# A hybrid decoder block on one core: another order of the seven products in closing Strassen steps, and the convolution's product four steps later

## The chip, the cores and the metric

The kernel runs on 1 core of one Trainium2 chip. The metric is the device time of one execution in microseconds (us), the median over the runs; lower is better.

## The reference

One decoder block on x of 256 tokens by 4096 channels in float32. Six kinds of projection come out of one matrix `w_in`; a pooling branch and a convolution branch are built from them, each goes through its own 2048x4096 matrix, sigmoid gates merge the two, and `w_out` and a norm close the block.

```python
h = rmsnorm(x, norm_w)
proj = h @ w_in                                   # 256 x 4096 by 4096 x 20480
u_p, z_p, u_c, b_c, c_c, z_c, g_logit = split(proj)
y_pool = (pooled(u_p) @ pool_w per group) * pool_scale * silu(z_p)   # trailing windows 2, 4, 8, 16
v = c_c * u_c
y_conv = b_c * (conv_b + sum(conv_w[k] * v shifted by 2-k, k = 0..2)) * silu(z_c)
br = [y_pool @ w_branch[0], y_conv @ w_branch[1]]  # each 256 x 2048 by 2048 x 4096
merged = sum(sigmoid(g_logit + gate_b) * br)
x = x + merged @ w_out                            # 256 x 4096 by 4096 x 4096
return rmsnorm(x, final_norm_w)
```

## The kernel before

**Units.** All the matrix work is cut into 31 units of 1024 output columns, one behind another. In order: `cz0 cb0 cu0 cc0 cz1 cb1 cu1 cc1` (the convolution branch: z, b, u and c projections of its two halves), `pz0 pu0 pz1 pu1` (the pooling branch), `g0_0 g0_1 g1_1 g0_2 g1_2 g0_3 g1_3 g1_0` (gates), `b0_0 b1_0 ... b0_3 b1_3` (branch matrices) and `o0 o1 o2 o3` (`w_out`). A unit is a row of 16 steps (8 in the `b` units). A step takes 256 rows of the weights: a 2x2 grid of 128x512 blocks, multiplied by a 2x2 grid of 128x128 blocks of the activations (two token halves by two row halves).

**Steps.** Every float32 operand is split into a rounded high part (type fp32r) and the rest, the low part, and a product is three matmuls: high by high, high by low, low by high. A P step does the eight block products plainly: 24 matmuls, into four PSUM banks, the E banks (t, n) for token half t and column half n, named `sums_82` (0,0), `sums_83` (0,1), `sums_84` (1,0) and `sums_85` (1,1). An S step does one round of Strassen's scheme in seven products: 21 matmuls, into three E banks (all but (1,0)) and four further banks, the F banks `shared_86` to `shared_89`. Three of the seven, N6, N4 and N7, need sums of weight blocks that VectorE (DVE) forms first (tile `parts`). Strings such as `"PPPPSPSPSSPSSPSS"` (L38 to L51) give each unit's steps; an S step that ends a unit is a *closing* step.

**Preparing a step.** SyncE loads the weights (`raw`: 768 KB, and a corner of 256 KB; for an S step GpSimd adds a second block into the corner by an accumulating DMA). ScalarE (ACT) writes the high parts into cells of `ring` (26 cells of 128x512), DVE the low parts, and in an S step DVE forms `parts`, ACT their highs (`ring<-parts`), DVE their lows. A step's cells are handed out in the order of the program, up to four steps ahead, where cells are free (`pump`, L1049).

**Closing a unit.** After each product, `after_group` (L1102) looks which banks are complete. A complete E bank is copied out by ACT at once (`evacuate`, L425: `E<-sums` or `Y<-sums`), a complete F bank by ACT into tile `J` (`copy_corners`, L431: `J<-shared`). These copies stand in ACT's queue in the order in which the banks close, among the high parts of the following steps. Every unit begins with a P step, which writes E bank (0,1) with its first three matmuls, (1,1) with the next three, then (0,0) and (1,0); a bank can be written again when its copy is done.

**Epilogues.** What a unit still has to do on ACT, DVE and the DMA queues is put into a queue of small items, one per *tick* of 6 matmuls (`tick`, L1084), so that it runs beside the next unit. Of `cc0` and `cc1` these are transposes, the taps of the convolution (`taps`, L590) and in the end `whole` (L605), the product of convolution and gate, `E<-J,Y`, four times 128x512. `gate_unit` (L718) puts two DMAs that add the bias rows (`E<-in_rows_dram`, GpSimd's queue) and 12 ticks later two sigmoids on ACT. `side_items` (L553) makes two extra Strassen operands of x after `cz0`.

**Operands.** The activations' operands for the `b` and `o` units come back from DRAM (`fills`, `Fill.advance`, L820): a transfer into a stage (`sa`, `sb`, `sc`), for an S operand four sums on DVE into a scratch tile `four` (one, the lower half of `sa`), highs on ACT (`arena<-`), lows on DVE.

**Start and end.** 18 matmuls of zeros (`WARM`, L33, L922) keep TensorE (PE) busy before the first weights arrive. At the end, `finish_half` (L1244) adds a half of the last columns and squares it, `finish` (L1251) forms the inverse root of the mean square and scales four tiles, which go out by DMA; it is done for token half 0, then for 1.

Of the kernel before, what the change touches and what calls it, by code (L numbers as in the profile page):

```python
# [54 lines left out]
def hybrid_block(ctx: ExitStack, tc: tile.TileContext, x, xc, prm, rows_in, w_in, pool_w, w_branch, w_out, out):  # L55
# [208 lines left out]
    class Step:  # L264
# [85 lines left out]
        def groups(self):  # L350
            gs = []
            if self is steps[0]:
                for k in (1, 0):
                    for n in (1, 0):
                        h, l, free = self.plain(2 * (1 - k) + 1 - n)
                        for i in range(3):
                            for t in range(2):
                                ah, al = self.op.standing(k, t)
                                gs.append([("E", t, n), [((ah, h), (al, h), (ah, l))[i]], ()])
                        gs[-1][2] = free  # L360
            elif self.kind == "P":
# [140 lines left out]
    def gap(n):  # L502
        return [None] * n
# [24 lines left out]
    def seq_x(text):  # L528
        if text is FIRST:
            return [("P", i) for i in FIRST]  # L530
        text = [c for c in text if c in "PS"]
        ns = text.count("S")
        if ns > NS + NB:
            ss = list(range(ND, 16)) + [resident[0]]
            if ns > NS + NB + 1:
                resident[0] = 2 * ND - 3 - resident[0]
                ss = [ss[-1]] + ss[:-1] + [resident[0]]
            ps = [i for i in range(ND) if i not in ss]
            return [(c, (ss if c == "S" else ps).pop(0)) for c in text]
        return sequence(text, ND, ND + NS + NB, NB)  # L540
# [9 lines left out]
    def side_load(i):  # L550
        aside(side["tile"], side_d[i - ND + 2])

    def side_items(i):  # L553
        def scaled():
            for k in range(2):
                v = sa[:, 6 - 2 * k:8 - 2 * k]
                act(v, v, scale=norm_col(2 * i + k))

        return [lambda: move(sa[:, 4:].rearrange("p o c -> p (o c)"), xc[i])] + gap(7) + [scaled, None, lambda: sums_s(sa)] + gap(3) + [
            lambda: act(side["tile"][:, 0], sa[:, 0:4]), None,  # L560
            lambda: sub(side["tile"][:, 1], sa[:, 0:4], side["tile"][:, 0].bitcast(F32)),
            None, None, None, None, lambda: aside(side_d[i - ND + 2], side["tile"])]

    def silu_y(late):
        def silu(t):
# [7 lines left out]
    def conv_units(c, first):  # L573
        base = 2 * HALF + c * NU

        def b_epi(u):
            def product(t):
                stt(E[:, t], E[:, t], rin[:, t:t + 1], Y[:, t], ALU.mult, ALU.mult)
            return gap(15) + [lambda: product(0), None, lambda: product(1)] + gap(5) + [lambda: move(g_d[c], E)]

        def c_epi(u):
            def inner(j):
                if j == 3:
                    for i in range(4):
# [28 lines left out]
        u = in_unit(f"cz{c}", base + 3 * HALF, lambda u: silu_y(u.late) + (gap(4) + side_items(ND - 1) + side_items(ND - 2) if first else []),  # L613
                    FIRST if first else EIGHT4, dst=Y)
        u.late = not first
        in_unit(f"cb{c}", base + HALF, b_epi, TEN if c else NINE_A).late = True
# [157 lines left out]
    def out_unit(c):  # L774
# [15 lines left out]
        text = (SEVEN4, NINE, NINE, OUT3)[c]  # L790
# [19 lines left out]
    class Fill:  # L810
        def __init__(self, o, src, free, ready):
            self.o, self.free, self.ready, self.src = o, free, ready, src
            self.at = self.st = None
            self.phase = self.due = 0

        def fetch(self, st):
            self.at, self.st = now[0], st
# [2 lines left out]
        def advance(self, force):  # L820
            o, q = self.o, self.st
            n = o.n - 4 if o.kind == "S" else 0
            four = sa[:, 0:4]
            if self.phase == 0 and n and any(f.phase and f.o.kind == "S" for f in fills):
                return False
            if not force and (now[0] < self.due or (self.phase != 1 and now[0] < quiet[0])):
                return False
            if self.phase == 0 and o.kind == "S":
# [20 lines left out]
                rested[id(self.st)] = now[0] + REST  # L849
            return True  # L850

    stages = [sa[:, 4:8]]
    fills = deque()
    now, quiet, hush = [0], [0], [0]
    LANDING, STORED, QUIET, HUSH, REST = 8, 7, 5, 20, 5
# [312 lines left out]
    for u in units:  # L1168
        if u.name == "b0_0":
            last_pair["stack"].close()  # L1170
            open_last(F32)
        if u is names["o1"]:
            assert not fills
            more.close()
            open_side()

# [11 lines left out]
        if u is last_x:  # L1188
            side["stack"].close()
            more = ExitStack()  # L1190
            ctx.enter_context(more)
            pool = more.enter_context(tc.tile_pool(name="more", bufs=1))
            apart["tile"] = pool.tile([P, 8 * P], F32R, name="apart")
            stages.extend(pool.tile([P, 4, P], F32, name=name) for name in ("sb", "sc"))
            queue_fills()
        if u is last:
            break
# [46 lines left out]
    def finish_half(t, n):  # L1244
# [3 lines left out]
            accum_out=ossq[:, t, 3 + n:4 + n])  # L1248
        mul(rest[:, t, cs], E[:, t, cs], Y[:, 0, cs])

    def finish(t):  # L1251
# [11 lines left out]
    for t in range(2):  # L1263
        for ns in ((0, 1),) if t == 0 else ((0,), (1,)):
# [49 lines left out]
```

## Time and profile before

| | |
|---|---|
| median of 3 runs | 2348.76 us (2348.66 to 2349.11) |
| the profiled execution's own time | 2348.53 us |
| its span, first to last instruction | 2346.8 us |
| granted TensorE clock | 0.999 |
| instructions in the trace | 29867 |

A row of the timeline says: start in us from the span's start, length in us, engine (PE is TensorE's matmuls, PEld its weight loads), line, operation, out<-in, shape, how many of them were merged into the row, and in brackets how long the engine idled before it and what ended that. A matmul row's length runs to the modelled end of its last matmul (389 ns for one of 512 columns), while the next begins earlier: the pace is read from starts, or from a row of many. Line 1096 is the helper `multiply`, lines 62 and 65 the helpers of ACT and of DVE, so the names of the tiles tell what a row is.

### The profile page before, as it was taken

The numbers are of one execution on the slowest core, as the hardware profiler recorded it, in microseconds if no ns is written. First come the engines' busy times: TensorE is split into PE (matmuls) and PEld (weight loads), VectorE is DVE, ScalarE is ACT, GpSimd is POOL, SyncE is SP. The second block draws the span as 40 slices with busy tenths as digits, with TensorE's granted clock in tenths as the row PEclk, the third lists the DMA queues.
The fourth block names the chain that finished last, engine by engine and source line by source line (L and its number), as shares of the span: only waits on it lengthen the run. The fifth ranks groups of instructions, "written<-read, shape, count | busy, mean of one in ns | idle before, by whom it ended". The sixth has DMA issues, their size and how long they took to land.

```text
span 2346.8 us, 29867 instructions
## 1 busy us (share of the span) xinstructions
PE 2332.0 (99%) x10382; PEld 1930.1 (82%) x10382; DVE 2134.0 (91%) x2177; ACT 1539.8 (66%) x1926; POOL 298.7 (13%) x362
## 2 busy tenths in 40 slices
PE   9999999999999999999999999999999999999998
PEld 7888888888888888888888888888888888878886
DVE  8789999999989979979999899998999889999898
ACT  6666656666666656667766766666676667666664
POOL 0111101111101101101121111111011010011110
PEclk9999999999999999999999999999999999999999
DMA  9789978989978868868999999999889889889998
GB/s 376 247 250 291 273 229 248 282 246 284 271 219 256 264 201 252 257 205 255 290 275 276 307 284 284 278 309 288 277 271 279 273 266 295 272 237 303 290 268 288
DMA packets 203975, 634.60 MB, mean 270 GB/s; under 512 B 21424, under 2 KB 29872, under 8 KB 201008
## 3 DMA queue, kind: packets, MB, share of 16 engines
q1 hardware_dynamic: 134912, 485.42, 59.0%
q0 software_dynamic: 51264, 105.40, 24.7%
q10 hardware_dynamic: 17648, 41.87, 4.9%
q8 instruction: 81, 1.33, 0.2%
q14 instruction: 70, 0.57, 0.1%
HBM read 585.42 MB, written 25.17 MB: 260 GB/s over the span
## 4 chain that ended last, share of the span: by engine, by line
PE 95%; DVE 3%; ACT 1%; issue 1%; DMA 0%; DVEq 0%; SPq 0%; ACTq 0%
PE sums L1096 67%; PE shared L1096 26%; DVE ring L65 2%; PE shared L705 1%; PE shared L483 1%; DVE parts L65 1%; DVE E L65 0%; ACT ring L62 0%; DVE Y L77 0%; DMA raw<-in_w_in_dram 0%; ACT J L62 0%; DVE raw L1259 0%; PE shared L681 0%; ACT Y L62 0%; PE shared L682 0%
## 5 line engine op out<-in xcount | busy, mean ns | idle before, releaser
L1096 PE MATMUL sums<-ring,arena 128*128 128x512 f32 x6732 | 1611.3, 390 | 2.9 <-ACT arena L62 1.3
L1096 PEld LDWEIGHTS sums<-ring,arena 128*128 128x128 f32 x6732 | 1262.2, 188 | 267.2 <-DVE ring L65 2.9
L65 DVE TENSOR_TENSOR ring<-raw,ring 128x512 fp32r<-128x512 f32 (+2 forms) x979 | 1091.8, 1140 | 143.9 <-PE sums L1096 57.5
L62 ACT ACTIVATE ring<-raw 128x512 fp32r<-128x512 f32 (+1 forms) x942 | 899.3, 1015 | 89.6 <-PE sums L1096 65.0
L62 ACT ACTIVATE ring<-parts 128x1024 fp32r<-128x1024 f32 (+1 forms) x493 | 399.7, 823 | 542.8 <-DVE parts L65 487.7
L1096 PE MATMUL shared<-ring,arena 128*128 128x512 f32 x2319 | 590.1, 389 | 0.0
L1096 PEld LDWEIGHTS shared<-ring,arena 128*128 128x128 f32 x2319 | 435.3, 188 | 90.3
L65 DVE TENSOR_TENSOR ring<-parts,ring 128x1536 fp32r<-128x1536 f32 (+2 forms) x274 | 416.7, 1533 | 4.8 <-ACT ring L62 4.6
L92 POOL DMA_DIRECT2D raw<-in_w_in_dram x178 | 153.9, 864 | 1369.2 <-DMA raw<-in_w_in_dram 518.1
L65 DVE TENSOR_TENSOR parts<-raw,parts 128x1024 f32<-128x1024 f32 x236 | 288.5, 1222 | 0.0
L65 DVE TENSOR_TENSOR parts<-raw 128x512 f32<-128x512 f32 x236 | 162.9, 690 | 2.2
L65 DVE TENSOR_TENSOR J<-J 128x512 f32<-128x512 f32 (+1 forms) x90 | 78.3, 870 | 15.1 <-ACT J L62 12.5
L62 ACT ACTIVATE E<-sums 128x512 f32<-128x512 f32 x76 | 42.1, 596 | 47.1 <-PE sums L1096 46.1
L62 ACT ACTIVATE J<-shared 128x512 f32<-128x512 f32 x128 | 68.3, 620 | 6.6 <-PE shared L1096 6.4
L1096 PE MATMUL sums<-ring,last_pair 128*128 128x512 f32 x261 | 66.1, 389 | 0.0
L1096 PE MATMUL shared<-ring,side 128*128 128x512 f32 x261 | 66.0, 389 | 0.0
L1096 PE MATMUL shared<-ring,last_pair 128*128 128x512 f32 x252 | 63.6, 389 | 0.0
L92 POOL DMA_DIRECT2D raw<-in_w_out_dram x33 | 28.7, 870 | 273.8 <-DVE ring L65 142.5
L92 POOL DMA_DIRECT2D raw<-in_w_branch_dram x25 | 21.7, 869 | 287.7 <-DVE ring L65 69.0
L1096 PEld LDWEIGHTS shared<-ring,side 128*128 128x128 f32 x261 | 49.0, 188 | 10.2
L1096 PEld LDWEIGHTS sums<-ring,last_pair 128*128 128x128 f32 x261 | 49.0, 188 | 10.2
L1096 PEld LDWEIGHTS shared<-ring,last_pair 128*128 128x128 f32 x252 | 47.3, 188 | 9.8
(133 smaller groups left out, 729.6 us busy)
## 6 DMA issues: line engine op xcount, KB each, us to landing
raw<-in_w_in_dram SPq DMA_DIRECT2D x318, 768.0 KB, 6.9
raw<-in_w_in_dram SPq DMA_DIRECT2D x326, 256.0 KB, 6.0
raw<-in_w_branch_dram SPq DMA_DIRECT2D x64, 768.0 KB, 7.2
raw<-in_w_out_dram SPq DMA_DIRECT2D x64, 768.0 KB, 7.1
raw<-in_w_in_dram POOLq DMA_DIRECT2D x178, 256.0 KB, 6.7
raw<-in_w_branch_dram SPq DMA_DIRECT2D x64, 256.0 KB, 5.6
raw<-in_w_out_dram SPq DMA_DIRECT2D x64, 256.0 KB, 6.0
E<-J POOLq DMA_DIRECT2D x30, 512.0 KB, 10.3
```

The lines of the kernel that those rows point to most:

```text
L62: return pin(nc.scalar.activation(dst, src, func, **kw))
L65: return pin(nc.vector.tensor_tensor(out=dst, in0=a, in1=b, op=op))
L92: return pin(nc.gpsimd.dma_start(dst, src, accum_op=ALU.add))
L483: pin(nc.tensor.transpose(shared(j)[:, i * T + t * P:i * T + (t + 1) * P], src[:, t, c:c + P], ident))
L705: pin(nc.tensor.matmul(o, a, b, start=(k, i) == (0, 0), stop=(k, i) == (3, 2)))
L1096: pin(nc.tensor.matmul(ps, lhs, rhs, start=n == 0, stop=n == u.total[b] - 1))
```

## The change

Six things are changed; what is computed is the same.

1. Closing S steps multiply in the order M2 N3 M1 N5 N4 N7 N6 (before: M2 N3 N4 M1 N7 N5 N6). The three products of formed sums now come last, so E bank (1,1), which N4 completes, closes fifth and not third.
2. `whole`, the convolution's product, is queued later: gaps of 12, 2, 3, 3 items ahead of its four parts (before 2, 2, 2, 2).
3. `cb0` gets ten S steps (before nine), `o0` six (before seven). `cb0` therefore uses both extra operands of x, and `side_items` makes both with one chain of items.
4. During `b1_3` and `o0` the fills have three scratch tiles for sums (before one), two of them in the place of the tile `apart`, which is closed earlier.
5. `WARM` is 23 (before 18).
6. `finish` does part of the mean square ahead (`partial`, three small DVE instructions after the first half), folds the rest into the square root's bias and drops one multiplication.

```diff
-WARM = 18
+WARM = 23
...
-NINE_A = "PSPSSPSPSSPSPSPS"
+TEN_B = ("PSPSSPSSP", "SSPSSPS")
...
-SEVEN4 = "PPPPSPSPSPSPSSPS"
+SIX5 = "PPPPPSPSPSPSPSPS"
...
-                order = ("M2", "N3", "N4", "M1", "N7", "N5", "N6") if self.closing else (
+                order = ("M2", "N3", "M1", "N5", "N4", "N7", "N6") if self.closing else (
                     "N5", "M2", "N3", "M1", "N6", "N7", "N4")
...
+        if text is TEN_B:
+            ss = list(range(ND, 13)) + [ND - 1] + list(range(13, 16)) + [ND - 2]
+            ps = list(range(ND - 2))
+            return [(c, (ss if c == "S" else ps).pop(0)) for c in "".join(text)]
...
-            for j in range(4):
-                items += gap(2) + [lambda j=j: whole(j)]
-            return items + gap(5) + [lambda: put(y_d[1, c], chan(E))]
+            for j, n in enumerate((12, 2, 3, 3)):
+                items += gap(n) + [lambda j=j: whole(j)]
+            return items + gap(4) + [lambda: put(y_d[1, c], chan(E))]
...
-            four = sa[:, 0:4]
-            if self.phase == 0 and n and any(f.phase and f.o.kind == "S" for f in fills):
-                return False
+            if self.phase == 0 and n:
+                used = [f.four for f in fills if f.phase and f.o.kind == "S"]
+                self.four = next((q for q in fours if not any(q is u for u in used)), None)
+                if self.four is None:
+                    return False
+            four = self.four
...
+        if u is names["b1_3"]:
+            lone.close()
...
+            fours.extend(pool.tile([P, 4, P], F32, name=name) for name in ("sd", "se"))
...
+    def partial(t):
+        b, h = known[:, t, 0:1], known[:, t, 1:2]
+        pin(nc.vector.tensor_reduce(out=b, in_=ossq[:, t, 0:4], axis=mybir.AxisListType.X, op=ALU.add))
+        pin(nc.vector.tensor_scalar(out=b, in0=b, scalar1=1.0 / D, scalar2=EPS, op0=ALU.mult, op1=ALU.add))
+        pin(nc.vector.tensor_scalar(out=h, in0=b, scalar1=-0.5, scalar2=None, op0=ALU.mult))
+
     def finish(t):
         r = rout[:, t:t + 1]
-        rstd_of(ossq[:, t:t + 1], r, f"rout{t}")
+        b, h, q, s = (known[:, t, i:i + 1] for i in range(4))
+        act(s, ossq[:, t, 4:5], AF.Sqrt, scale=1.0 / D, bias=b)
+        stt(h, ossq[:, t, 4:5], -0.5 / D, h, ALU.mult, ALU.add)
+        pin(nc.vector.reciprocal(out=r, in_=s))
+        stt(q, r, h, r, ALU.mult, ALU.mult)
+        stt(r, q, 1.5, r, ALU.add, ALU.mult)
...
             for n in ns:
                 finish_half(t, n)
+            if 0 in ns:
+                partial(t)
         finish(t)
```

The change moves instructions. First, ScalarE's queue at the border from unit `g1_3` to `g1_0`, before: `E<-sums` are the copies of E banks, `J<-shared` of F banks, `ring<-raw` the high parts of a later step.

```order
L62 ACTIVATE E<-sums_83 128x512
L62 ACTIVATE E<-sums_82 128x512
L62 ACTIVATE E<-sums_85 128x512
L62 ACTIVATE J<-shared_86 128x512
L62 ACTIVATE J<-shared_88 128x512
L62 ACTIVATE J<-shared_87 128x512
L62 ACTIVATE ring<-raw 128x1536
L62 ACTIVATE ring<-raw 128x512
L62 ACTIVATE J<-shared_89 128x512
```

The same place in the changed kernel:

```order
L62 ACTIVATE E<-sums_83 128x512
L62 ACTIVATE E<-sums_82 128x512
L62 ACTIVATE J<-shared_86 128x512
L62 ACTIVATE J<-shared_87 128x512
L62 ACTIVATE ring<-raw 128x1536
L62 ACTIVATE ring<-raw 128x512
L62 ACTIVATE E<-sums_85 128x512
L62 ACTIVATE J<-shared_88 128x512
L62 ACTIVATE J<-shared_89 128x512
```

The copy of bank `sums_85` has moved from the third place to the seventh, behind two copies of F banks and, here, behind the two instructions that make the high parts of a later step. At the border from `g1_0` to `b0_0` it stands behind the same four; from `b0_3` to `b1_3` behind two copies and an `arena<-sb`; at the other borders behind a closing S step behind the two copies alone.

Second, VectorE's queue in the middle of `cz1`, before; `E<-J,Y` is `whole`, `ring<-raw` and `ring<-parts` are low parts.

```order
L65 TENSOR_TENSOR E<-J,Y 128x512
L65 TENSOR_TENSOR parts<-raw 128x512
L65 TENSOR_TENSOR ring<-raw,ring 128x512
L65 TENSOR_TENSOR parts<-raw,parts 128x1024
L65 TENSOR_TENSOR E<-J,Y 128x512
L65 TENSOR_TENSOR ring<-raw,ring 128x1536
L65 TENSOR_TENSOR ring<-parts,ring 128x1536
L65 TENSOR_TENSOR ring<-raw,ring 128x1536
L65 TENSOR_TENSOR ring<-raw,ring 128x512
L65 TENSOR_TENSOR E<-J,Y 128x512
L65 TENSOR_TENSOR parts<-raw 128x512
```

The same steps in the changed kernel:

```order
L65 TENSOR_TENSOR parts<-raw 128x512
L65 TENSOR_TENSOR ring<-raw,ring 128x512
L65 TENSOR_TENSOR parts<-raw,parts 128x1024
L65 TENSOR_TENSOR ring<-raw,ring 128x1536
L65 TENSOR_TENSOR ring<-parts,ring 128x1536
L65 TENSOR_TENSOR ring<-raw,ring 128x1536
L65 TENSOR_TENSOR ring<-raw,ring 128x512
L65 TENSOR_TENSOR parts<-raw 128x512
L65 TENSOR_TENSOR ring<-raw,ring 128x512
L65 TENSOR_TENSOR parts<-raw,parts 128x1024
L65 TENSOR_TENSOR E<-J,Y 128x512
```

The second S step of the pair (its `parts`, then `ring<-raw` of 1536 and `ring<-parts`) and the P step behind it have no `whole` among them any more; the first `whole` stands in the S step that follows.

More of the change, by code (lines that the diff above doesn't have):

```diff
@@ L551, in side_load, with side_items, fetch, made @@
         aside(side["tile"], side_d[i - ND + 2])
[L553 to L562, printed above, removed]
+    def side_items(a, b):
+        def fetch(i):
+            return lambda: move(sa[:, 4:].rearrange("p o c -> p (o c)"), xc[i])
+        def made(i):
+            def scaled():
+                for k in range(2):
+                    v = sa[:, 6 - 2 * k:8 - 2 * k]
+                    act(v, v, scale=norm_col(2 * i + k))
+            def high():
+                st = next(s for s in steps[16:] if s.op is x_ops[a] and s.kind == "S")
+                assert i == a or state["now"] > steps.index(st)
+                act(side["tile"][:, 0], sa[:, 0:4])
+            return [scaled, None, lambda: sums_s(sa)] + gap(3) + [
+                high, None, lambda: sub(side["tile"][:, 1], sa[:, 0:4], side["tile"][:, 0].bitcast(F32))]
+        def keep(i):
+            return lambda: aside(side_d[i - ND + 2], side["tile"])
+        return [fetch(a)] + gap(7) + made(a) + [fetch(b)] + gap(3) + [keep(a)] + gap(3) + made(b) + gap(4) + [keep(b)]
     def silu_y(late):
@@ L607, in whole @@
                 mul(chan(E)[:, b], chan(J)[:, b], chan(Y)[:, b])
-            for j in range(4):
-                items += gap(2) + [lambda j=j: whole(j)]
-            return items + gap(5) + [lambda: put(y_d[1, c], chan(E))]
-        u = in_unit(f"cz{c}", base + 3 * HALF, lambda u: silu_y(u.late) + (gap(4) + side_items(ND - 1) + side_items(ND - 2) if first else []),
+            for j, n in enumerate((12, 2, 3, 3)):
+                items += gap(n) + [lambda j=j: whole(j)]
+            return items + gap(4) + [lambda: put(y_d[1, c], chan(E))]
+        u = in_unit(f"cz{c}", base + 3 * HALF, lambda u: silu_y(u.late) + (gap(4) + side_items(ND - 1, ND - 2) if first else []),
                     FIRST if first else EIGHT4, dst=Y)
         u.late = not first
-        in_unit(f"cb{c}", base + HALF, b_epi, TEN if c else NINE_A).late = True
+        in_unit(f"cb{c}", base + HALF, b_epi, TEN if c else TEN_B).late = True
         u = in_unit(f"cu{c}", base, lambda u: rescale(Y), TEN, dst=Y)
@@ L788, in epi @@
                 lambda: mul(E, E, Y[:, 0:1].to_broadcast([P, 2, NU]))] + gap(4) + [lambda: move(o_d[c], E)]
-        text = (SEVEN4, NINE, NINE, OUT3)[c]
+        text = (SIX5, NINE, NINE, OUT3)[c]
         u = Unit(f"o{c}", lambda i: w_out[c, i], seq_x(text), m_ops, epi, before=start if c == 3 else None)
@@ L814, in __init__ @@
             self.phase = self.due = 0
+            self.four = None
         def fetch(self, st):
@@ L850, in advance @@
             return True
-    stages = [sa[:, 4:8]]
+    stages, fours = [sa[:, 4:8]], [sa[:, 0:4]]
     fills = deque()
@@ L1171, in hybrid_block @@
             open_last(F32)
+        if u is names["b1_3"]:
+            lone.close()
+            lone = ExitStack()
+            ctx.enter_context(lone)
+            pool = lone.enter_context(tc.tile_pool(name="lone", bufs=1))
+            fours.extend(pool.tile([P, 4, P], F32, name=name) for name in ("sd", "se"))
         if u is names["o1"]:
             assert not fills
+            lone.close()
             more.close()
@@ L1192, in hybrid_block @@
             pool = more.enter_context(tc.tile_pool(name="more", bufs=1))
-            apart["tile"] = pool.tile([P, 8 * P], F32R, name="apart")
             stages.extend(pool.tile([P, 4, P], F32, name=name) for name in ("sb", "sc"))
+            lone = ExitStack()
+            ctx.enter_context(lone)
+            apart["tile"] = lone.enter_context(tc.tile_pool(name="lone", bufs=1)).tile([P, 8 * P], F32R, name="apart")
             queue_fills()
```

1 line of the change is left out of this document (added).

## The prediction

> **What bounds the kernel now.** I read the page's busy times first, then PE's own waits, then the timeline at each place where PE loses time.
>
> ```profile
> span 2346.8 us, 29867 instructions
> PE 2332.0 (99%) x10382; PEld 1930.1 (82%) x10382; DVE 2134.0 (91%) x2177; ACT 1539.8 (66%) x1926; POOL 298.7 (13%) x362
> ...
> PE sums L1096 <- ACT arena L62: 1.3, 1, 1.3
> ...
> 24.01 9.00 PE L1096 MATMUL sums<-ring,arena 128*128 128x512 f32 x39
> ```
>
> PE is the bound: busy 99%, and the longest of its listed waits is 1.3 us. Its pace is (9.00 - 0.39)/38 = 0.2267 us for a matmul of 512 columns. Only two things can move the time: the number of matmuls, and moments in which PE loses time. DVE is close behind at 91%, so what delays DVE or ACT can become a new moment of that kind. All sums below are made against the profiled execution's own 2348.53 us (span 2346.8); the runs' median 2348.76 lies 0.23 above it, and I add that at the end. A measurement of this kernel can tell about 0.2%, 4.7 us, from no change.
>
> **The number of matmuls.** `cb0` gains an S step and `o0` loses one; each swap is 24 - 21 = 3 matmuls, 0.68 us, once down and once up: 0. DVE's load moves along (an S step has more lows and sums); in `cb0` it is covered by DVE's slack, and the `TEN` units already run ten S steps beside PE without a wait in the list.
>
> **Stalls that the change takes away.** In the timeline, PE and DVE in the middle of `cz1`, PE at the like place of `pz0`, then a step of `pz1` and one of `g0_0`, and the last step of `o0`:
>
> ```profile
> 385.61 0.70 DVE L65 TENSOR_TENSOR E<-J,Y 128x512 f32<-128x512 f32 x1
> 386.21 1.76 DVE L65 TENSOR_TENSOR ring<-raw,ring 128x1536 fp32r<-128x1536 f32 x1
> 387.37 0.39 PE L1096 MATMUL sums<-ring,arena 128*128 128x512 f32 x1
> 388.03 1.42 PE L1096 MATMUL sums<-ring,arena 128*128 128x512 f32 x5 [0.27 <-DVE ring L65]
> ...
> 713.92 0.39 PE L1096 MATMUL sums<-ring,arena 128*128 128x512 f32 x1
> 714.62 1.43 PE L1096 MATMUL sums<-ring,arena 128*128 128x512 f32 x5 [0.31 <-DVE ring L65]
> ...
> 923.51 1.14 PE L1096 MATMUL sums<-ring,arena 128*128 128x512 f32 x3
> ...
> 1102.19 1.19 PE L1096 MATMUL sums<-ring,arena 128*128 128x512 f32 x3
> ...
> 2082.78 3.11 PE L1096 MATMUL sums<-ring,last_pair 128*128 128x512 f32 x13
> 2085.97 0.61 ACT L62 ACTIVATE arena<-sa 128x512 fp32r<-128x512 f32 x1
> 2087.16 2.69 PE L1096 MATMUL sums<-ring,arena 128*128 128x512 f32 x9 [1.27 <-ACT arena L62]
> ```
>
> *cz1, pz0.* The second matmul of a product waits for lows that DVE ends at 386.21 + 1.76 = 387.97, because `whole` stood ahead of them. Loss: 388.03 - 387.37 - 0.23 = 0.43, and 1.42 - (0.39 + 4 x 0.2267) = 0.12 in the row itself: 0.55; in `pz0` 0.47 + 0.13 = 0.60. In the order three of the four `whole` (each 0.60 from start to start) now stand behind these lows, 1.8 us of room where 0.6 is missing. They come later among steps whose lead they shorten, but never beyond what it is today, since by the third S pair all four are done in either kernel. I take the whole gain, -1.15; bounds -1.15 and 0 (the stall comes back a step later).
>
> *pz1, g0_0.* Three matmuls should take 0.39 + 2 x 0.2267 = 0.84 and take 1.14 and 1.19: N4 waits for the lows of formed sums. N4 now comes two products (1.36 us) later: -0.30 - 0.35 = -0.65.
>
> *o0.* The 13 end their issue at 2082.78 + 13 x 0.2267 = 2085.73; the next starts at 2087.16 (1.43 late), and its nine take 2.69 instead of 2.20 (0.49): 1.92. The closing step's operand was filled last, its highs only at 2085.97, behind the one scratch tile. In the changed order its sums no longer wait for another fill to let go of that tile, and one S step less goes before it: for DVE one instruction of 1536 lows (1.76, as at 386.21) and the two that form `parts` less. I take -1.92; bounds -1.92 and -1.2, the second if DVE writes this fill's two lows (0.69 us each today) just too late.
>
> **The start.** PE's first rows, and the third step's weights:
>
> ```profile
> 1.12 4.02 PE L923 MATMUL shared<-warm 128*128 128x256 bf16 x18 [1.12 <-DVE warm L919]
> 6.02 16.11 PE L1096 MATMUL sums<-ring,arena 128*128 128x512 f32 x63 [0.88 <-DVE ring L802]
> ...
> 15.33 2.01 ACT L62 ACTIVATE ring<-raw 128x1536 fp32r<-128x1536 f32 x2 [1.78 <-DMA raw<-in_w_in_dram]
> 16.86 2.36 DVE L65 TENSOR_TENSOR ring<-raw,ring 128x1536 fp32r<-128x1536 f32 x2
> 18.67 1.46 PEld L1096 LDWEIGHTS sums<-ring,arena 128*128 128x128 f32 x7 [0.16 <-DVE ring L65]
> ```
>
> A warm-up matmul takes about 0.21 us, so five more fill the idle 0.88 us to within 0.2. The 63 real ones should take 0.39 + 62 x 0.2267 = 14.44 and take 16.11: 1.67 us lost, most of it in the first microseconds at half pace. The Trainium skill ("TensorE: Matmul & The Clock Gate", section "What's actually happening") says that the array runs at half clock until a free-running window of about 3.4 us was busy; by it a gap-free warm-up would release the clock about when the real work starts, and up to 1.5 us would go out of the sum. The trace agrees as far as it goes: behind the gap of 0.88 the work starts slow. I don't take that gain: the third step needs lows that DVE starts at 16.86 and ends 1.76 later, at 18.6, tied to a load whose landing ended ACT's wait at 15.33, and PE is there at 18.67 already with 0.16 of waiting. A faster first step waits there. -0.1; bounds -1.5 (if those loads also come earlier) and +0.2 (five extra at 0.21 against 0.88).
>
> **What the new order of products costs.** E bank (1,1) closes two products later, its copy goes to the back of ACT's queue, and the next unit's second product, three matmuls in, writes that bank. ACT and PE at three borders (`g1_3` to `g1_0`, `g1_0` to `b0_0`, `b0_3` to `b1_3`) and at that of `pz1`:
>
> ```profile
> 1585.22 1.56 ACT L62 ACTIVATE E<-sums 128x512 f32<-128x512 f32 x3
> 1586.65 1.59 ACT L62 ACTIVATE J<-shared 128x512 f32<-128x512 f32 x3
> 1588.08 2.05 ACT L62 ACTIVATE ring<-raw 128x1536 fp32r<-128x1536 f32 x2
> 1589.97 0.65 ACT L62 ACTIVATE J<-shared 128x512 f32<-128x512 f32 x1
> 1587.39 4.92 PE L1096 MATMUL sums<-ring,arena 128*128 128x512 f32 x21
> ...
> 1667.59 1.26 ACT L62 ACTIVATE E<-sums,rin 128x512 f32<-128x512 f32 x2
> 1668.73 0.70 ACT L62 ACTIVATE E<-sums,rin 128x512 f32<-128x512 f32 x1
> 1669.67 4.70 PE L1096 MATMUL sums<-ring,arena 128*128 128x512 f32 x20
> ...
> 1960.74 2.00 ACT L62 ACTIVATE ring<-raw 128x512 fp32r<-128x512 f32 x2
> 1962.64 0.59 ACT L62 ACTIVATE E<-sums 128x512 f32<-128x512 f32 x1
> 1964.81 3.56 PE L1096 MATMUL sums<-ring,arena 128*128 128x512 f32 x15
> ...
> 925.38 1.55 ACT L62 ACTIVATE Y<-sums 128x512 f32<-128x512 f32 x3
> 927.23 1.98 PE L1096 MATMUL sums<-ring,arena 128*128 128x512 f32 x8
> ```
>
> From start to start a copy takes 0.48 (1585.22 to 1586.65 in three), one scaled by `rin` 0.57, the pair of highs 1.89 (1588.08 to 1589.97). Queued behind the copy and so late with it: the last two `J` copies and the highs of the next step; PE waits for the copy itself.
>
> *g1_3:* copies at 1585.22 and 1585.70, `J` at 1586.17 and 1586.65, highs from 1587.13 to 1589.02, then bank (1,1), done 0.6 later at 1589.6. PE wants it at 1587.39 + 0.68 = 1588.07: +1.55. *g1_0:* copies at 1667.59 and 1668.16, `J` at 1668.73 and 1669.21, highs to 1671.58, copy done at 1672.28, wanted at 1670.35: +1.93. *b0_3:* an `arena` high of 0.5 now ahead of the highs puts the first copy at 1963.16, the second at 1963.64, `J`, `J` and another `arena` follow, the copy starts at 1965.6 and ends at 1966.2, wanted at 1965.49: +0.70. *pz1, g0_0:* copies from 925.38, bank (1,1) fifth, at 925.38 + 4 x 0.48 = 927.3, done at 927.9, wanted at 927.23 - 0.30 + 0.68 = 927.61: +0.3 each, which eats the gain there. *cc0, cc1:* as `g1_0` without the highs, 1.93 - 1.89: +0.1 for both. At the other borders the same count ends before PE asks. Sum +4.9. No row of the trace shows PE waiting for such a copy; bounds 0, if ACT gets to these copies earlier than today, and +6, if each is late by a further 0.1 to 0.2.
>
> **The end.** DVE's second half add, ACT's root and the scaling of the last half:
>
> ```profile
> 2336.05 0.68 DVE L65 TENSOR_TENSOR E<-sums,E 128x512 f32<-128x512 f32 x1
> ...
> 2337.72 0.15 DVE L930 TENSOR_SCALAR rout_m<-rout_m 128x1 f32<-128x1 f32 x1
> 2337.91 0.20 ACT L62 ACTIVATE rout_s<-rout_m 128x1 f32<-128x1 f32 x1 [0.41 <-DVE rout_m L930]
> ...
> 2338.92 1.54 DVE L1259 TENSOR_SCALAR raw<-raw,rout 128x512 f32<-128x512 f32 x3
> ```
>
> Small DVE instructions stand 0.19 apart. Two before the root and one behind it go: -0.6. But for token half 1 the three of `partial` stand in DVE's queue ahead of the add at 2336.05, and PE has that half done by then (DVE is the late one): +0.6. The sum is 0; bounds -0.4 and +0.3.
>
> **The sum.** -1.15 - 0.65 - 1.92 - 0.1 + 4.9 + 0 = +1.1 us: 2349.6 for an execution like the profiled one, 2349.9 for the median.
>
> **The rivals.**
>
> *The copies cost nothing.* For it: ACT idles a third of the time. Against: at these borders it has no idle row, it runs copies and highs back to back. Sum -3.8: 2345.0. Still within 0.2%.
>
> *The same, and a full pace from the first matmul is kept.* If the array, busy without a gap, runs at full pace from 6.02 and the third step's load lands as much earlier, the 1.67 lost go, less the 0.16 of waiting and up to 0.2 of longer warm-up: -1.3 more, 2343.7, faster. The row at 18.67 speaks against it.
>
> *Slower: the bias rows.* GpSimd's queue, the profile's DMA issues and ACT in `g1_3`:
>
> ```profile
> 1549.20 1.19 POOL L92 DMA_DIRECT2D E<-in_rows_dram  x1
> E<-in_rows_dram POOLq DMA_DIRECT2D x14, 512.0 KB, 10.3
> 1559.66 1.99 ACT L62 ACTIVATE E<-E 128x1024 f32<-128x1024 f32 x2
> ```
>
> In six gate units one corner load now stands ahead of both bias transfers, so both start where the second did, and the second lands later. Today it lands at about 1549.2 + 10.3 = 1559.5, and its sigmoid starts at 1560.6. If it lands a whole transfer after the first, at 1569.8, ACT stands some 5 us with the highs behind it. Cover: the order also puts that sigmoid four highs (about 4 us) further back, to 1564.6, and PE's lead over the lows takes up 2 more. It decides from a landing 7 us after the first; then about 3 us in each of six units: 2368.
>
> *The change doesn't do what it says:* the three waits on lows and fills stay or come back next door, the copies cost as above: +1.1 + 3.7 = +4.8: 2353.6, just slower.
>
> **How the numbers follow.** Forecast 0.72, free copies 0.13, free copies and clock 0.05, bias rows 0.04, stalls that stay 0.06. Likeliest: 2349.9. From 2344.9 to 2353.0 the range holds the forecast with its bounds (about 2347.5 to 2352) and the free copies; the last three cases lie outside. Faster by over 0.2% is the clock case, 0.05; slower is the bias rows and most of the last, 0.08; the rest, 0.87, is within 0.2%.
>
> **What would show it.** Right: in the profile after, PE waits for `E<-sums` or ACT at the starts of `g1_0`, `b0_0` and `b1_3`, 1.5, 1.9 and 0.7 us, and the gaps at 387, 714 and 2087 us are gone; the first 63 matmuls end as today, with a wait for DVE in the third step. Wrong: no PE gap at those starts; a third step that starts a microsecond earlier; sigmoids that wait for `E<-in_rows_dram`; or a time beyond the range.

## The result, and the profile after

| | before | after |
|---|---|---|
| median, each of 5 runs side by side | 2348.80 us | 2358.76 us (2357.97 to 2359.44) |
| ratio, with its 95% interval | | 1.004 (1.0028 to 1.0052) |
| the profiled execution's own time | 2348.53 us | 2357.97 us |
| its span | 2346.8 us | 2356.2 us |

The kernel became 0.4% slower. The forecast was 2349.9, within 0.2% of before, with a range up to 2353.0: wrong, by 8.9 us.

From the page of the changed kernel, the busy times and the two groups of matmuls that take their weights from `last_pair` (count, busy time, mean ns of one, idle time ahead):

```profile
span 2356.2 us, 29866 instructions
PE 2338.0 (99%) x10387; PEld 1929.2 (82%) x10387; DVE 2134.1 (91%) x2166; ACT 1541.7 (65%) x1918; POOL 294.9 (13%) x362
...
L1116 PE MATMUL sums<-ring,last_pair 128*128 128x512 f32 x261 | 68.7, 396 | 0.5 <-DVE ring L65 0.3
L1116 PE MATMUL shared<-ring,last_pair 128*128 128x512 f32 x252 | 65.9, 397 | 0.0
```

The same two groups on the page of before:

```profile
L1096 PE MATMUL sums<-ring,last_pair 128*128 128x512 f32 x261 | 66.1, 389 | 0.0
...
L1096 PE MATMUL shared<-ring,last_pair 128*128 128x512 f32 x252 | 63.6, 389 | 0.0
```

PE is busy 6.0 us more with five warm-up matmuls more and no real one: the 513 matmuls of the two groups take longer, 396 to 397 ns in the mean instead of 389. What PE waits for, of the changed kernel:

```profile
PE sums L1116 <- ACT E L62: 3.9, 3, 1.8
PE sums L1116 <- DVE ring L65: 1.6, 2, 1.3
PE shared L943 <- DVE warm L939: 1.1, 1, 1.1
```

The first row is the forecast's late copies; the wait for `arena`, 1.3 us before, is gone. PE and ACT at the starts of `g1_0`, `b0_0` and `b1_3`, where the prediction put them:

```profile
1593.61 0.62 ACT L62 ACTIVATE E<-sums 128x512 f32<-128x512 f32 x1
...
1594.29 3.03 PE L1116 MATMUL sums<-ring,arena 128*128 128x512 f32 x12 [1.47 <-ACT E L62]
...
1678.13 0.71 ACT L62 ACTIVATE E<-sums,rin 128x512 f32<-128x512 f32 x1
...
1678.89 1.45 PE L1116 MATMUL sums<-ring,arena 128*128 128x512 f32 x5 [1.81 <-ACT E L62]
...
1975.06 1.20 PE L1116 MATMUL sums<-ring,arena 128*128 128x512 f32 x4 [0.62 <-ACT E L62]
```

A unit's length, from its first matmul's start to the next unit's, is the finest measure of all: worked out from the starts in the trace, it repeats to 0.02 us from one execution to another where nothing waits (80.24 in every undisturbed unit of 354 matmuls). The differences, after less before:

| term | forecast | measured |
|---|---|---|
| a step on `last_pair` in 24 of the 32 units (80.24 became 80.43) | none | 24 x 0.193 = +4.6 |
| late copy, `g1_0`, `b0_0`, `b1_3` | +1.55 +1.93 +0.70 | +1.79 +2.15 +0.82 |
| late copy, starts of `cz1 pz0 cb1 pu0 pu1 g0_1` | +0.7 (0.1 for `cz1 pz0`, 0.6 for `pu1 g0_1`) | +1.81 (0.53, 0.62, and 0.66 for `cb1 pu0`) |
| waits inside `cz1` and `pz0` | -1.15 | -0.14 |
| N4 in `pz1` and `g0_0` | -0.65 | -0.78 |
| last step of `o0` | -1.92 | -1.85 |
| start and `cz0`, less its step on `last_pair` | -0.1 | +0.70 |
| from the last product to the end | 0 | +0.3 |

These and +0.09 of `b1_1` come to +9.5, and so do the spans (2356.25 less 2346.77). The list of units ahead of the prediction has 32 names, not 31. In a unit with no wait at all, `cu1`, the 21 matmuls of the step on `last_pair`, before:

```profile
566.78 0.84 PE L1096 MATMUL sums<-ring,arena 128*128 128x512 f32 x3
567.46 0.84 PE L1096 MATMUL shared<-ring,last_pair 128*128 128x512 f32 x3
568.14 1.52 PE L1096 MATMUL sums<-ring,last_pair 128*128 128x512 f32 x6
569.50 2.20 PE L1096 MATMUL shared<-ring,last_pair 128*128 128x512 f32 x9
571.54 0.84 PE L1096 MATMUL sums<-ring,last_pair 128*128 128x512 f32 x3
```

And after:

```profile
568.66 0.62 PE L1116 MATMUL sums<-ring,arena 128*128 128x512 f32 x2
569.12 0.86 PE L1116 MATMUL shared<-ring,last_pair 128*128 128x512 f32 x3
569.82 1.56 PE L1116 MATMUL sums<-ring,last_pair 128*128 128x512 f32 x6
571.22 2.28 PE L1116 MATMUL shared<-ring,last_pair 128*128 128x512 f32 x9
573.34 0.86 PE L1116 MATMUL sums<-ring,last_pair 128*128 128x512 f32 x3
```

From the first matmul on `last_pair` to the nineteenth it takes 571.54 - 567.46 = 4.08 before (0.2267 for each of 18) and 573.34 - 569.12 = 4.22 after (0.234). No row has a wait in brackets, and the order of the products in this step isn't changed: it isn't a closing step.

What did change is where `last_pair` lies. The tiles made by `sb` stand in a pool that is filled from the top of the memory. The new tile `known` takes 32 bytes per partition there, and four small tiles of the old `finish` (32 each) are no longer made: everything below moved up by 96 bytes. In the two built programs `last_pair` starts at byte 167008 instead of 166912 = 326 x 512. A filler tile, `sb("back", [P, 40])`, stood in that pool all along.

### The profile page after: what moved, and what is told of

It reads as the page before. It is cut to its first block, busy times and chain, and to the rows that moved or that the text cites. A ratio compares the mean times of both kernels' runs of the same rounds, so it can differ in the third digit from the quotient of the medians.

```text
span 2356.2 us, 29866 instructions
## 1 busy us (share of the span) xinstructions
PE 2338.0 (99%) x10387; PEld 1929.2 (82%) x10387; DVE 2134.1 (91%) x2166; ACT 1541.7 (65%) x1918; POOL 294.9 (13%) x362
## 3 DMA queue, kind: packets, MB, share of 16 engines
q8 instruction: 81, 1.33, 0.2%
## 4 chain that ended last, share of the span: by engine, by line
PE 96%; DVE 2%; ACT 1%; DMA 1%; issue 0%; SPq 0%; DVEq 0%
PE sums L1116 67%; PE shared L1116 27%; PE shared L721 1%; DVE ring L65 1%; PE shared L483 1%; DMA raw<-in_w_in_dram 1%; ACT ring L62 0%; DVE E L65 0%; DVE parts L65 0%; ACT E L62 0%; DVE raw L1301 0%; PE shared L697 0%; ACT J L62 0%; PE shared L698 0%; PE shared L700 0%
## 5 line engine op out<-in xcount | busy, mean ns | idle before, releaser
L62 ACT ACTIVATE ring<-raw 128x1536 fp32r<-128x1536 f32 (+2 forms) x936 | 900.4, 1022 | 112.6 <-PE sums L1116 72.8
L1116 PE MATMUL shared<-ring,side 128*128 128x512 f32 x270 | 70.9, 389 | 0.0
```

The costliest lines, as they stand in the source:

```text
L62: return pin(nc.scalar.activation(dst, src, func, **kw))
L1116: pin(nc.tensor.matmul(ps, lhs, rhs, start=n == 0, stop=n == u.total[b] - 1))
```

## The experiments

Each is compared with runs of the kernel before on the same chip (its median was 2349.18, 2349.11 and 2349.34 in the three sets). **Two theories** for the slow matmuls: *place*, the address of `last_pair`, against *order*, the new order of the closing products. For the waits at the borders: *late copies*.

### The changed kernel at the old addresses

```diff
-    sb("back", [P, 40])
+    sb("back", [P, 64])
```

> The changed kernel with `back` 64 instead of 40 words wide, which puts `last_pair` and every tile of that pool back at the addresses that they have in the kernel before (they had moved up by 96 bytes, to 32 beyond a multiple of 64). Theory 'place': the 513 matmuls that take their weights from `last_pair` (509 of them stand 234 ns behind the one before instead of 227) go back to 227 ns, -3.8 us: 2355.0; and if the opening loads land later for the same reason, the first product starts at 6.02 again and the third step's lows end at 18.6 instead of 19.3: -0.7 more, 2354.3. Rival 'order': the slow matmuls come from the new order of the closing products; then the mean of that group stays 396 to 397 ns and the time 2358.8.

Measured 2354.16, 1.0015 times before (1.0005 to 1.0024). From its page:

```profile
L1116 PE MATMUL sums<-ring,last_pair 128*128 128x512 f32 x261 | 67.1, 390 | 0.5 <-DVE ring L65 0.3
L1116 PE MATMUL shared<-ring,last_pair 128*128 128x512 f32 x252 | 64.0, 389 | 0.0
```

The matmuls are back at 389 to 390 ns, `cu0` at 80.24, and 4.6 us are gone with a filler tile. *Order* has fallen for them. That the start came back for the same reason is not shown: the first product starts at 6.05, but the third step's lows end at 19.05, and `cz0` is no shorter than `last_pair` accounts for (89.39 to 89.16).

### The kernel before, moved by 32, 64 and 128 bytes

```diff
-    sb("back", [P, 40])
+    sb("back", [P, 32])
```

(24 and 8 words in the two others.)

> The kernel before with `back` 32 instead of 40 words wide: all tiles of that pool, `last_pair` among them, start 32 bytes higher, and nothing else changes. 'Place': the mean of the matmuls with weights from `last_pair` goes from 389 to 396 or 397 ns, +3.8 us, 2352.6, and perhaps 0.2 to 0.9 more at the start if the opening loads land later too. 'Order': no change, 2348.8.

> The kernel before with `back` 24 words wide: the pool's tiles start 64 bytes higher, 64 beyond a multiple of 512. If a start at a multiple of 64 bytes is enough, the matmuls with weights from `last_pair` keep 389 ns and the time stays 2349.2; if it takes a multiple of 128 or of 512 (a weight row is 512 bytes), they have 396 ns and the time is 2353.

> The kernel before with `back` 8 words wide: the pool's tiles start 128 bytes higher, 128 beyond a multiple of 512. If starts at multiples of 128 are enough, the matmuls with weights from `last_pair` have 389 ns and the time is 2349.1; if it takes 256 or 512, they have 395 to 396 ns and the time is 2352.8.

Measured 2352.95, 1.0012 (1.0003 to 1.0021); 2352.92, 1.0020 (1.0011 to 1.0029); 2352.34, 1.0014 (1.0005 to 1.0022). The page's row of the first, of the second and of the third:

```profile
L1096 PE MATMUL sums<-ring,last_pair 128*128 128x512 f32 x261 | 67.9, 396 | 0.0
```

```profile
L1096 PE MATMUL sums<-ring,last_pair 128*128 128x512 f32 x261 | 67.9, 396 | 0.0
```

```profile
L1096 PE MATMUL sums<-ring,last_pair 128*128 128x512 f32 x261 | 67.5, 394 | 0.0
```

So *place* makes the kernel before slower by 3.0 to 3.8 us (medians; the intervals are some 2 us to either side) with nothing else changed, and neither a multiple of 64 nor one of 128 is enough.

### The kernel before with the new order alone

```diff
-                order = ("M2", "N3", "N4", "M1", "N7", "N5", "N6") if self.closing else (
+                order = ("M2", "N3", "M1", "N5", "N4", "N7", "N6") if self.closing else (
```

> The kernel before with the new order of the closing products alone. 'Late copies': the waits at the starts of g1_0, b0_0 and b1_3 (1.7, 2.1 and 0.9 us in the changed kernel) and six small ones of 0.29 appear, 6.4 us, less the 0.65 of the N4 waits: 2354.5. 'Place': the matmuls on `last_pair` stay at 389 ns. 'Order' would add their 3.8 us: 2358.3. If the waits need the other edits as well: 2348.2.

Measured 2355.76, 1.0022 (1.0013 to 1.0031). `last_pair` stays at 389 ns. What PE waits for:

```profile
PE sums L1096 <- ACT E L62: 4.3, 3, 1.8
PE sums L1096 <- DVE ring L65: 1.9, 3, 1.3
PE sums L1096 <- ACT arena L62: 1.3, 1, 1.3
```

The three waits for the copy are there without any other edit, though not quite in the same places: the third, 1.0, is at `b1_1` (1.44 longer as a unit), and `b1_3` is 0.32 longer. Of the six small ones four are there, 1.56 together; `cb1` and `pu0` stay at 80.24 and 80.92, so their late copies need another of the edits as well, and no run says which. The whole came out 1.3 above the expectation: 0.4 of it is the kernel before, slower on this chip, and about 0.9 the waits of `b1_1` and `b1_3`, for which 0.9 had been taken and 1.8 came. The profiled execution, 2357.36, has 1.6 more for a cause that nobody had expected, told at the end: behind the wait of `b0_0` eight matmuls went at half pace.

### Everything but the order, at the old addresses

The changed kernel with `back` 64 and the old line for the order.

> The changed kernel with the old addresses (`back` 64) and the old order of the closing products; the other edits stay. By 'place' and 'late copies' together: 2358.8 - 3.8 - 6.4 + 0.65 = 2349.2, and the last step of o0 still without its 1.9 us wait; the waits of cz1 and pz0 (0.4 and 0.6) stay where the changed kernel has them, in the closing step. If the other edits by themselves cost time: over 2351.

Measured 2349.72, 0.9998 (0.999 to 1.0007), half a microsecond above the expectation. No late copy is left, and `o0` is as short as in the changed kernel (85.05). But `b1_3` has grown from 41.57 to 43.57, which the new order had hidden. PE, then DVE, around it:

```profile
1970.98 0.39 PE L1116 MATMUL sums<-ring,arena 128*128 128x512 f32 x1
1973.15 1.20 PE L1116 MATMUL sums<-ring,arena 128*128 128x512 f32 x4 [1.78 <-DVE ring L65]
```

```profile
1961.45 0.69 DVE L65 TENSOR_TENSOR arena<-sa,arena 128x512 fp32r<-128x512 f32 x1
1965.81 0.69 DVE L65 TENSOR_TENSOR arena<-sb,arena 128x512 fp32r<-128x512 f32 x1 [3.67 <-ACT arena L62]
1966.42 0.68 DVE L65 TENSOR_TENSOR parts<-raw 128x512 f32<-128x512 f32 x1
```

A fill's low (`arena<-sb`) stands at the head of DVE's queue and waits 3.67 us for its high, which ACT has behind the copies of the closing unit; a step's lows stand behind it. Two places remain where the cost can come from: the new scratch tiles or the moved S step.

### The scratch tiles alone, and the moved step alone

The first adds `fours` and `lone`, the second `TEN_B` with its `side_items` and `SIX5`, each to the kernel before.

> The kernel before with the second and third scratch tile for the fills alone (`fours`, `lone`). Theory 'given back next door': o0 loses its wait of 1.65 (86.02 to 84.4), but at the border of b0_3 and b1_3 the fill now taken up early puts its low in DVE's queue ahead of a step's lows, and its high in ACT's queue behind the bank copies: b1_3 goes from 41.57 to 43.5 as in the run with the old order, 2349.5. Rival: that wait in b1_3 came with the shorter o0 list, b1_3 stays at 41.6: 2347.5.

> The kernel before with the moved S step alone (`TEN_B` in cb0 with its reload of the side tile, `SIX5` in o0); one scratch tile for the fills as before, the old order, `whole`, start and tail. Read by unit lengths: cb0 80.92 to 80.24 (three matmuls less). Theory 'one fill less is enough': o0's last step loses its wait, o0 goes from 86.02 to 85.05 though it has three matmuls more, and the time is 2349.2 - 0.68 - 0.97 = 2347.5. Rival 'the second scratch tile did it': the wait stays, o0 is 86.7 and the time 2349.2. b1_3 stays at 41.57 in both.

The scratch tiles: 2349.35, 1.0001 (0.9992 to 1.0009). The time is as the theory had it, and both theories are wrong all the same: `b1_3` stays (41.58), and `o0` loses only 0.17. The moved step: 2351.96, 1.0014 (1.0006 to 1.0023), against 2347.5 or 2349.2. `cb0` is 0.68 shorter as reckoned, but `o0` has 86.32 (a wait of 0.93 is left), `b1_3` has the 43.57, and `cz1` and `pz0` have grown to 86.51 and 86.25. So neither part alone frees `o0`, while with both it has 85.05 (the run above), and the moved step costs 3.1 in three units that it doesn't touch.

### Half a tick

One thing that a step moves without touching: the items of the queue are paced by a counter of six matmuls, and three fewer in `cb0` leave it half a tick off until `o0`. At the end of those two units:

```diff
+        if u is names["cb0"] or u is names["o0"]:
+            state["mm"] += 3
```

once in the kernel before, and once with the moved step and the scratch tiles.

> The kernel before, the counter put three matmuls on at the ends of cb0 and o0, and nothing else. 'Half a tick': the units between show the losses of the run with the moved step: cz1 85.81 to 86.5, pz0 85.86 to 86.25, b1_3 41.57 to 43.5; about 2352. 'Place in the ring': the units stay as they are, 2349.1.

> The kernel before with the moved S step and the scratch tiles (`TEN_B`, `SIX5`, `fours`, `lone`), and the counter that paces the queued items (one item per six matmuls, `TICK`) put three matmuls on at the ends of cb0 and o0, where a step that has three matmuls less or more had moved it by half a tick. Theory 'half a tick': the new wait of b1_3 (1.95) goes and the waits of cz1 and pz0 return to 0.43 and 0.47; o0 has no wait (both parts are there): cb0 80.24, cz1 85.8, b1_3 41.6, o0 85.05, 2349.1 - 0.68 - 0.97 = 2347.5. Rival 'place in the ring': the waits come from the other places of the tiles in the ring, which the counter doesn't set: cz1 86.5, pz0 86.3, b1_3 43.6, 2350.6.

In the kernel before, 2349.82, 1.0002 (0.9993 to 1.001): `cz1` 86.41 and `pz0` 86.33 with no step moved, as the theory had it; but `b1_3` stays at 41.54 where the theory had 43.5, and so the time is not the 2352 expected. PE in `cz1`:

```profile
387.15 0.39 PE L1096 MATMUL sums<-ring,arena 128*128 128x512 f32 x1
388.31 0.98 PE L1096 MATMUL sums<-ring,arena 128*128 128x512 f32 x3 [0.77 <-DVE ring L65]
```

That is the wait of 0.27 that the prediction quotes at 388.03, 0.5 longer. With the moved step and the counter set right: 2348.02, 0.9997 (0.9988 to 1.0005); `cz1` 85.90, `pz0` 85.75, `cb0` 80.24, `o0` 84.78, and 42.69 in `b1_3`. So half a tick is the whole cost in `cz1` and `pz0`. In `b1_3` it costs nothing by itself, and setting it right took away 0.9 of the moved step's 2.0 (the scratch tiles were there too); what holds the other 1.1 stays open (the places in the ring, or the fills' list).

### The first P step takes bank (1,1) last

```diff
+            elif self.kind == "P" and self is self.unit.steps[0]:
+                for k in (1, 0):
+                    for n, t in ((1, 0), (0, 0), (0, 1), (1, 1)):
```

added to the changed kernel at the old addresses.

> The changed kernel with the old addresses, and the first P step of each unit takes its products in the order of banks (0,1), (0,0), (1,0), (1,1) instead of (0,1), (1,1), (0,0), (1,0), so bank (1,1) is written two products (1.36 us) later. 'Late copies': the waits at the starts of g1_0, b0_0 and b1_3 go from 1.63, 1.97 and 0.78 to 0.3, 0.6 and 0, those of 0.3 to 0.5 at the six other borders vanish: about -5.9, from 2354.2 to 2348.3, and b0_0 has no matmuls at half pace behind its wait. Rival: PE then waits as long for lows of the other cells or for a copy of another bank: 2354.

Measured 2348.78, 0.9998 (0.9989 to 1.0007). PE at the start of `b0_0`:

```profile
1669.82 1.75 PE L1122 MATMUL sums<-ring,arena 128*128 128x512 f32 x7
1672.05 2.14 PE L1122 MATMUL sums<-ring,arena 128*128 128x512 f32 x8 [0.48 <-ACT E L62]
```

The gap between two starts beyond 0.2267 went from 1.97 in the changed kernel to 0.64 there and from 1.63 to 0.27 in `g1_0`, that is by 1.33 and 1.36 for two products of 0.68 each; the six small ones are gone or at 0.1 to 0.2. `b1_3` waits 0.3 for DVE instead of 0.6 for the copy. PE waited for this copy: *late copies* is shown.

### A version from the parts that pay

The moved step, the scratch tiles and the counter on the kernel before, and the new order in `pz1` and `g0_0` alone, with the first P step of the units behind them as in the last run.

> As the run with the moved step, the scratch tiles and the counter, and besides the new order of the closing products in pz1 and g0_0 alone, with the first P step of the units behind them taking bank (1,1) last. pz1 97.79 to 97.45, g0_0 97.80 to 97.40, pu1 80.92 to 81.1, g0_1 80.24 to 80.44: -0.4 against that run, 2347.1 by 'half a tick', 2350.2 by 'place in the ring'.

Measured 2347.78, 0.9993 (0.9984 to 1.0001). `pz1` 97.40, `g0_0` 97.41, `pu1` 81.11 and `g0_1` 80.46 are as expected. The median is below that of both kernels, but the interval still holds no change against before.

## Why the prediction was wrong, step by step

**The end** is the step that failed most, and with it a sentence of the first paragraph: "Only two things can move the time: the number of matmuls, and moments in which PE loses time." A third moved it: the pace of 513 matmuls, 0.234 us instead of 0.2267. The prediction priced the new `partial` and `finish` by their instructions, and there it was nearly right (0 forecast, +0.3 measured, 0.0 to 0.3 in the changed kernels at the old addresses). It did not ask where the new tile `known` and the small tiles that are dropped would put the others. That is +4.6, more than the 3.1 from the forecast to the range's upper end, and no rival had it. The diff shows the tiles, but no address; the two built programs do. It is not the only step that failed: at the old addresses the changed kernel's median is 2354.2, still 1.2 above the range.

**The late copies** were the right mechanism, named with the right units, and too small: 6.6 against 4.9. At the three big borders each was 0.1 to 0.25 longer, because a wait has a tail: the matmul behind it loses 0.11 more, and a few after that some ns each. The sentence that failed is "At the other borders the same count ends before PE asks": `cb1` and `pu0` start 0.32 and 0.34 late. At `cz1` and `pz0` it is 0.53 together instead of 0.1; `pu1` and `g0_1` were right (0.62 against 0.6). The upper bound (+6) nearly held the sum.

**Stalls in `cz1` and `pz0`** took the wrong end of its own bounds. The wait at 387 and 714 went and came back in the closing step, where DVE is now as late. PE in `pz0` of the changed kernel:

```profile
745.46 0.40 PE L1116 MATMUL sums<-ring,last_pair 128*128 128x512 f32 x1
746.20 1.44 PE L1116 MATMUL sums<-ring,last_pair 128*128 128x512 f32 x5 [0.35 <-DVE ring L65]
```

DVE does the same work in these units, and the wait moved instead of going: nearly the bound of 0 ("the stall comes back a step later"). That the later `whole` moved it is argued, since no run has that edit alone. That the size of these waits hangs on half a tick had not been seen at all.

**`pz1`, `g0_0` and `o0`** were right (-0.78 and -1.85 against -0.65 and -1.92). For `o0` the prediction named the second tile and the S step less together, and the runs show that both are needed: neither does it alone.

**The number of matmuls** was right at 0 for `cb0` and `o0`, but its cover was wrong: three matmuls more or less also shift every queued item behind them by half a tick. In the changed kernel this is mixed with the later `whole`; in the kernel before it costs 1.1.

**The start** was right in its reason and unlucky in its size. PE and ACT of the changed kernel:

```profile
6.24 11.83 PE L1116 MATMUL sums<-ring,arena 128*128 128x512 f32 x49
...
16.02 2.01 ACT L62 ACTIVATE ring<-raw 128x1536 fp32r<-128x1536 f32 x2 [2.33 <-DMA raw<-in_w_in_dram]
...
19.36 0.50 PE L1116 MATMUL sums<-ring,arena 128*128 128x512 f32 x1 [1.29 <-DVE ring L65]
```

Forty-nine matmuls take 11.83 us where 0.39 + 48 x 0.2267 = 11.27 would be ideal, none at half pace, and the last of them starts 1.0 us ahead of before's (17.57 against 18.54); PE then waits for the third step's lows. The load landed at 16.02 instead of 15.33, and that is scatter: in the fourteen profiled executions it landed between 14.55 and 16.02, whatever `WARM` was. In the nine of them that had at most one matmul at half pace, the fiftieth starts 0.05 to 0.06 us behind the end of those lows: they set it, not PE's pace. By the Trainium skill ("TensorE: Matmul & The Clock Gate", section "What's actually happening") the full clock comes after a busy window of about 3.4 us; as an estimate from that, a warm-up without a gap would release it about when the work starts. The trace agrees: of the four executions with 23 warm-up matmuls three had no half-paced matmul at the start and one had one; of the ten with 18, five had 6 to 9 and five none. The moments of the switch to full clock, which the traces hold too, say the same: 5.85 to 7.12 us in the four, and in the ten either 3.86 to 5.21 or, behind the gap, 9.33 to 10.41. The gain is lost in the same wait, as the forecast said.

**The rivals.** The stalls that stay (2353.6) came nearest, by luck: at the old addresses the changed kernel takes 2354.2, but of that rival's 3.7 only the stalls of `cz1` and `pz0` (1.0) came back next door; larger copies and the start make up the rest. The copies were not free. The full pace from the first matmul did come, but the third step's load did not come earlier with it. The bias rows cost nothing: the gate units without a late copy are longer by the 0.19 of `last_pair` alone.

## What to carry to other kernels

A new or dropped tile is an edit to the address of every tile behind it: compare the addresses of both builds before costing an edit at its instructions, and start tiles of matmul weights at multiples of 512 bytes, the only starts that kept the pace here. When a product closes a bank later, count the copies of that bank through ACT's queue at every border, and make the next unit write that bank last; that reorder of the first P step took back 5.4 us of what the other order had cost. And where queued work is paced by a count of instructions, a change of that count moves all work behind it: a wait that appears in units the edit doesn't touch is looked for there.

## What the runs showed of the hardware

**Weights off 512 bytes are slower.** The mean distance between two matmuls with weights from `last_pair`, by where the tile starts beyond a multiple of 512 bytes:

| start beyond a multiple of 512 | ns between starts | a unit of 80.24 us grows by | 24 such units |
|---|---|---|---|
| 0 (before) | 226.7 | | |
| 32 | 233.0 | 0.17 us | 4.0 us |
| 64 | 233.4 | 0.15 | 3.7 |
| 96 (the changed kernel) | 234.1 | 0.19 | 4.6 |
| 128 | 232.4 | 0.12 | 2.9 |

A weight block is 128x128 in float32, 512 bytes per partition; the other tiles of weights (`arena`, `side`, `extra`, `apart`) start on such multiples in both built programs and kept their pace (`arena` 226.8 and 226.9, `side` 226.8 and 226.8). The profile's mean of a weight load stays at 188 ns in all of these, so whether the load or the matmul gets slower is open, and so is 256. The Trainium skill ("SBUF — State Buffer", section "Operand start alignment") asks only for a multiple of the element's size and says that its runs timed nothing; for the speed of weights these runs ask for more.

**A wait of under 2 us can halve the clock.** In two executions the wait of `b0_0` was followed by eight matmuls at half pace; in the changed kernel's own, the same wait was not. The windows behind it (PE's busy time and instructions, those of the other engines, then the granted clock), of the changed kernel at the old addresses:

```profile
1676.00:1679.40 3.40, 3.40 (x10) 2.61 (x9) 1.91 (x3) 2.95 (x5) 0.00 (x0) 0.54 0.96 290
```

And of the changed kernel itself:

```profile
1679.50:1683.00 3.50, 3.50 (x17) 2.87 (x16) 2.16 (x3) 3.14 (x5) 0.00 (x0) 1.00 0.90 303
```

The clock is 0.54 against 1.00 after an idle time of 1.83 and of 1.81 us. The unit took 45.89 instead of 44.31, so a wait of this length costs 2.1 or 3.7 us. The Trainium skill ("TensorE: Matmul & The Clock Gate", section "What's actually happening") has the slow state come after an idle window of about 3.4 us, free-running. The length of the half pace, eight matmuls of 0.43, agrees with that window; an idle time of 1.83 us that brings it on is shorter than the Trainium skill has it.

The moments at which the clock switched tell the two waits apart. In the execution at the old addresses it went to full at 7.12 us, to half at 1676.24 and to full again at 1679.65; these are 489 and 1 times 3.413 us, so the switches lie on a fixed grid. There the whole wait (1673.54 to 1675.54, counting 0.2267 us for each matmul) lay in the window that ended at 1676.24. In the changed kernel's own, with switches at 5.85 and 2347.39 (686 times 3.413), a window ended at 1678.38, in the middle of the wait from 1676.91 to 1678.89. Counted like this over all windows of the fourteen traces that began at full clock, those with up to 1.88 us without a matmul were not followed by half pace, and those with 2.11 us or more were.
